# Dealing row pairs to partitions so that the 16 DMA engines read neighbouring pairs, in a mean over rows

## The chip, the cores and the metric

The kernel runs on one core of one Trainium2 chip; the other cores are idle. Times are device microseconds (us) of that core, medians of several executions. The median of before is 1245.4 us (1245.29 to 1245.93 in four runs).

## The reference

```python
"x": np.random.randn(64, 256, 8192).astype(np.float32)
def reference(x): return np.mean(x, axis=2)
```

That is 16384 rows of 32 KiB, 537 MB to read, and 64 KiB of means to write. It is a problem of reading memory.

## The kernel before

A tile is 256 rows: partition p of 128 receives the row pair p of the tile, 64 KiB in one piece. Three buffers in SBUF, the memory on the chip, rotate. SP (SyncE) issues the loads, 16 DMA engines carry them out, DVE (VectorE) sums each row, TensorE transposes the sums at the end into PSUM, its output memory, and ACT (ScalarE) copies them out of there in order. A packet is the piece that one DMA engine moves at a time; the trace records each (8064 of 64 KiB for the full tiles; while they move, 16 are in flight for 97.7% of the time). The last 256 rows come in ever smaller pieces, so that little work is left after the last byte.

```python
P, R, NBUF = 128, 2, 3                     # L = 8192
x_rows = x.rearrange("b c l -> (b c) l")
x_pair = x_rows.rearrange("(t p r) l -> t p (r l)", p=P, r=R)
out_pair = out.rearrange("b c -> (b c)").rearrange("(t n) -> t n", n=R * P)
# ... cut: buffers, semaphores
def sync_program(eng):
    for t in range(NP):                    # NP = 63 full tiles
        if t >= NBUF:
            eng.wait_ge(dve_sem, t - NBUF + 1)
        eng.dma_start(bufs[t % NBUF][:], x_pair[t]).then_inc(in_sems[t % NBUF], 16)
    # ... cut: six loads of the last tile, two stores
def vector_program(eng):
    def pair(k, trip, dst):
        eng.wait_ge(in_sems[k], trip)
        eng.tensor_reduce(dst, bufs[k][:].rearrange("p (r l) -> p r l", r=R), X, ADD
                          ).then_inc(dve_sem, 1)
    # ... cut: the loop over tiles, the last tile
def scalar_program(eng):
    for r in range(R):
        eng.wait_ge(pe_sem, r + 1)
        eng.activation(outsb[:, :, r], ps[r][:], Copy, scale=inv).then_inc(cp_sem, 1)
    # ... cut: the last tile
def tensor_program(eng):
    eng.wait_ge(prep_sem, 4)
    eng.wait_ge(dve_sem, NP + 1)
    for r in range(R):
        eng.transpose(ps[r][:], res[:, :, r], ident[:]).then_inc(pe_sem, 1)
    # ... cut: the last tile
```

Of the kernel before, what the change touches and what calls it, by code (L numbers as in the profile page):

```python
# [6 lines left out]
def bass_global_avg_pool_1d_kernel(  # L7
# [4 lines left out]
    P = 128  # L12
    B, C, L = x.shape
    rows = B * C
    inv = 1.0 / float(L)
# [3 lines left out]
    Copy = mybir.ActivationFunctionType.Copy  # L19



    R = 2
    assert rows % (R * P) == 0
    NP = rows // (R * P) - 1
    NBUF = 3
# [6 lines left out]
    BLOCKS.append((32, [L // 8, 5 * L // 64, 3 * L // 64]))  # L33
    assert sum(n for n, _ in BLOCKS) == R * P
    assert all(sum(ch) * P == n * L for n, ch in BLOCKS)
# [2 lines left out]
    NCH = sum(len(ch) for _, ch in BLOCKS)  # L38

    x_rows = x.rearrange("b c l -> (b c) l")  # L40
    x_pair = x_rows.rearrange("(t p r) l -> t p (r l)", p=P, r=R)
    out_pair = out.rearrange("b c -> (b c)").rearrange("(t n) -> t n", n=R * P)

    with ExitStack() as ctx:
        E = ctx.enter_context
        bufs = [E(nc.sbuf_tensor(f"buf{i}", [P, R * L], f32)) for i in range(NBUF)]
        res = E(nc.sbuf_tensor("res", [P, NP, R], f32))
# [5 lines left out]
        outsb = E(nc.sbuf_tensor("outsb", [NP, P, R], f32))  # L53
        lastsb = E(nc.sbuf_tensor("lastsb", [1, R * P], f32))
        ps = [E(nc.psum_tensor(f"ps{r}", [NP, P], f32)) for r in range(R)]
# [8 lines left out]
        cp_sem = E(nc.semaphore("cp_sem"))  # L64
# [103 lines left out]
        def scalar_program(eng):  # L168

            for r in range(R):  # L170
                eng.wait_ge(pe_sem, r + 1)
                eng.activation(outsb[:, :, r], ps[r][:], Copy, scale=inv).then_inc(cp_sem, 1)  # L172
            at = 0
            for k, (n, _) in enumerate(BLOCKS[:-1]):
                eng.wait_ge(pe_sem, R + 1 + k)
                eng.activation(lastsb[:, at : at + n], psb[k][:, :n], Copy).then_inc(cp_sem, 1)  # L176
                at += n
# [17 lines left out]
        gpsimd_program(nc.gpsimd)  # L195
        vector_program(nc.vector)
        scalar_program(nc.scalar)
        tensor_program(nc.tensor)

# [39 lines left out]
```

## Time and profile before

| | before |
|---|---|
| median time, us | 1245.4 |
| GB/s over the span | 432 |
| one full tile (8.39 MB), us | 19.39 |
| DVE on one full tile, us | 17.22 |
| packets of the full tiles | 8064 of 64 KiB |
| one such packet, mean / median, us | 2.424 / 2.421 |

From the page of before: the busy share of DVE and of the DMA engines in 40 slices (tenths), the rate in each slice, the costliest group of instructions (count, busy us, mean ns, idle time before and what ended it), and the loads (count, median us from issue to landing). Then the shares of the chain of work that ended last.

```profile
DVE  2898988989889888898898988989889898898988
DMA  9999999999999999999999999999999999999998
GB/s 436 415 430 438 438 438 426 417 438 438 438 438 438 436 407 438 438 438 438 438 434 409 438 438 438 438 438 434 409 438 438 438 438 438 432 411 438 438 438 373
DMA packets 10010, 536.94 MB, mean 432 GB/s; under 512 B 1114, under 2 KB 1306, under 8 KB 1562
...
L130 DVE TENSOR_REDUCE res<-buf 128x16384 f32 (+1 forms) x62 | 1067.6, 17220 | 152.4 <-DMA buf<-in_x_dram 152.4
...
buf<-in_x_dram SPq DMA_DIRECT2D x63, 40.7
...
DMA 70%; DVE 29%; issue 0%; SPq 0%; DVEq 0%; PE 0%
```

DMA is busy to the end and DVE idles 152.4 us waiting for it, so the loads bound the kernel. A load lands 40.7 us after its issue, twice a tile's 19.39: one tile always queues behind the one being moved. The dips to 407-417 are no stalls. The trace shows the 16 engines starting their packets within 0.46 us of one another (in 99 of 100 rounds), so bytes arrive in rounds of 16 x 64 KiB, and a slice of 31.1 us counts 12 or 13 of them; 13 rounds make 438 GB/s. Two longer windows (columns: stretch and its length, busy us and instructions of each engine, clock, DMA share, GB/s) show no dip; the second is the last tile:

```profile
400.00:1200.00 800.00, 0.00 (x0) 0.00 (x0) 712.69 (x42) 0.00 (x0) 0.00 (x0) 1.00 1.00 434
1222.10:1242.50 20.40, 2.68 (x14) 0.80 (x14) 18.29 (x16) 1.16 (x5) 0.00 (x0) 1.00 0.92 389
```

### The profile page before, as it was taken

What the parts mean: (1) busy time and instruction counts of PE and PEld (TensorE: products, weight loads), DVE (VectorE), ACT (ScalarE), POOL (GpSimd) and SP (SyncE); (2) the same over time, 40 slices, a digit from 0 to 9 for tenths busy, and PEclk for the clock granted to TensorE, in tenths of its full rate; (3) what the DMA queues carried; (4) which work ended last, traced back from release to release, by engine and by line L of the source; (5) the groups of instructions that cost most, each with busy time, mean ns of one, the idle gap of its engine ahead of it and who ended that gap; (6) DMA issues with size and microseconds to landing.
All of it is one profiled execution on the core that took longest, in us unless ns stands there. A gap on an engine that the chain in (4) does not pass through costs nothing.

```text
span 1243.9 us, 331 instructions
## 1 busy us (share of the span) xinstructions
PE 2.7 (0%) x14; PEld 0.8 (0%) x14; DVE 1086.1 (87%) x79; ACT 2.4 (0%) x6; POOL 1.2 (0%) x8
## 2 busy tenths in 40 slices
PE   0000000000000000000000000000000000000000
PEld 0000000000000000000000000000000000000000
DVE  2898988989889888898898988989889898898988
ACT  0000000000000000000000000000000000000000
POOL 0000000000000000000000000000000000000000
DMA  9999999999999999999999999999999999999998
GB/s 436 415 430 438 438 438 426 417 438 438 438 438 438 436 407 438 438 438 438 438 434 409 438 438 438 438 438 434 409 438 438 438 438 438 432 411 438 438 438 373
DMA packets 10010, 536.94 MB, mean 432 GB/s; under 512 B 1114, under 2 KB 1306, under 8 KB 1562
## 3 DMA queue, kind: packets, MB, share of 16 engines
q1 hardware_dynamic: 10010, 536.94, 99.9%
HBM read 536.87 MB, written 0.07 MB: 432 GB/s over the span
## 4 chain that ended last, share of the span: by engine, by line
DMA 70%; DVE 29%; issue 0%; SPq 0%; DVEq 0%; PE 0%
DMA buf<-in_x_dram 70%; DVE res L130 29%; DVEq L130 0%; SPq L113 0%; DVE buf L137 0%; SPq L109 0%; PE psb L188 0%; DVE lastsb L166 0%; DVE part L137 0%
## 5 line engine op out<-in xcount | busy, mean ns | idle before, releaser
L130 DVE TENSOR_REDUCE res<-buf 128x16384 f32 (+1 forms) x62 | 1067.6, 17220 | 152.4 <-DMA buf<-in_x_dram 152.4
L137 DVE CUSTOM_DVE_ANT_0 buf<-buf 128x4096 f32<-128x4096 f32 (+5 forms) x8 | 18.2, 2292 | 3.9 <-DMA buf<-in_x_dram 3.7
L183 PE MATMUL ps<-ident,res 128*63 128x128 f32 x2 | 0.7, 433 | 1231.1 <-DVE res L137 1231.1
L172 ACT ACTIVATE outsb<-ps 63x128 f32<-63x128 f32 x2 | 0.5, 279 | 1228.5 <-PE ps L183 1228.5
L188 PE MATMUL psb<-ind,part 128*1 128x32 f32 (+1 forms) x10 | 1.4, 238 | 4.1 <-DVE part L137 4.1
L172 ACT ACT_TABLE_LOAD x1 | 1.3, 1283 | 1.7 <-PEq L224 1.7
L183 PEld LDWEIGHTS ps<-ident,res 128*63 128x63 f32 x2 | 0.3, 202 | 1231.0 <-issue 1231.0
L176 ACT ACTIVATE lastsb<-psb 1x128 f32<-1x128 f32 (+2 forms) x3 | 0.7, 222 | 8.3 <-PE psb L188 8.3
L188 PE MATMUL psb<-ident,part 128*1 128x128 f32 x2 | 0.6, 397 | 4.6 <-DVE part L137 4.6
L137 DVE DVE_READ_ACCUMULATOR2_ANT part<- 128x1 f32 x6 | 0.5, 82 | 0.0
L166 DVE COPY lastsb<-psb 1x32 f32<-1x32 f32 x1 | 0.2, 178 | 0.4 <-PE psb L188 0.4
L188 PEld LDWEIGHTS psb<-ind,part 128*1 128x1 f32 x10 | 0.4, 80 | 5.5 <-DVE part L137 5.5
L85 POOL TENSOR_SCALAR_AFFINE_SELECT ident<-ident 128x128 f32<-128x128 f32 x1 | 0.3, 293 | 0.2 <-POOL ident L83 0.2
L95 POOL TENSOR_TENSOR ind<-ident 128x64 f32<-128x64 f32 x1 | 0.3, 291 | 0.1
L99 POOL TENSOR_TENSOR ind<-ind 128x32 f32<-128x32 f32 x1 | 0.2, 238 | 0.1
L83 POOL MEMSET ident<- 128x128 f32 x1 | 0.2, 204 | 1.3 <-POOLq L224 1.3
L137 DVE DVE_READ_ACCUMULATOR2_ANT res<- 128x1 f32 x2 | 0.2, 83 | 0.0
L224 POOL MEMSET const-bfloat16-1.0<- 128x1 bf16 x1 | 0.1, 101 | 0.0
L224 POOL MEMSET const-uint8-127<- 128x1 uint8 x1 | 0.1, 101 | 0.0
L224 POOL MEMSET const-float32-0.0<- 128x1 f32 x1 | 0.1, 98 | 0.2 <-issue 0.2
L224 POOL MEMSET const-float32-1.0<- 128x1 f32 x1 | 0.1, 98 | 0.0
L188 PEld LDWEIGHTS psb<-ident,part 128*1 128x1 f32 x2 | 0.1, 80 | 5.0 <-DVE part L137 5.0
## 6 DMA issues: line engine op xcount, KB each, us to landing
buf<-in_x_dram SPq DMA_DIRECT2D x1, 4096.0 KB, 31.1
buf<-in_x_dram SPq DMA_DIRECT2D x1, 2048.0 KB, 16.7
buf<-in_x_dram SPq DMA_DIRECT2D x1, 1024.0 KB, 18.8
buf<-in_x_dram SPq DMA_DIRECT2D x63, 40.7
buf<-in_x_dram SPq DMA_DIRECT2D x1, 512.0 KB, 19.6
buf<-in_x_dram SPq DMA_DIRECT2D x1, 320.0 KB, 20.0
buf<-in_x_dram SPq DMA_DIRECT2D x1, 192.0 KB, 20.0
out_dram<-outsb SPq DMA_DIRECT2D x1, 63.0 KB
```

The costliest lines, as they stand in the source:

```text
L83: eng.memset(ident[:], 0.0).then_inc(prep_sem, 1)
L85: eng.affine_select(out=ident[:], in_=ident[:], compare_op=mybir.AluOpType.not_equal, fill=1.0, base=0, pattern=[[-1, P]], channel_multipl ...
L95: eng.tensor_tensor(ind64[:], ident[:, 0:P:2], ident[:, 1:P:2], ADD).then_inc(prep_sem, 1)
L99: eng.tensor_tensor(ind32[:], ind64[:, 0:64:2], ind64[:, 1:64:2], ADD).then_inc(prep_sem, 1)
L130: eng.tensor_reduce(dst, bufs[k][:].rearrange("p (r l) -> p r l", r=R), X, ADD).then_inc(dve_sem, 1)
L137: return eng.tensor_tensor_reduce(out=run[:, 0:h], in0=run[:, 0:h], in1=run[:, h:], scale=scale, scalar=0.0, op0=ADD, op1=ADD, accum_out=dst,)
L166: eng.tensor_copy(lastsb[:, EARLY:], psb[-1][:, :n]).then_inc(last_sem, 1)
L172: eng.activation(outsb[:, :, r], ps[r][:], Copy, scale=inv).then_inc(cp_sem, 1)
L176: eng.activation(lastsb[:, at : at + n], psb[k][:, :n], Copy).then_inc(cp_sem, 1)
L183: eng.transpose(ps[r][:], res[:, :, r], ident[:]).then_inc(pe_sem, 1)
L188: mm = eng.matmul(psb[k][:, :n], part[:, i : i + 1], ind[n][:], start=start, stop=stop)
L224: nc = _bacc.Bacc("TRN2", target_bir_lowering=False, num_devices=1)
```

## The change

The intent: at any time the 16 engines should read 16 neighbouring pairs, 1 MiB of memory in one piece. The source pattern therefore deals the pairs as (j, e): partition 8e + j gets pair 16j + e. It supposes that the outer index e goes to the engines. The sums then stand in another order, which the two ACT copies undo.

```diff
     R = 2
+    J = P // 16
@@
-    x_pair = x_rows.rearrange("(t p r) l -> t p (r l)", p=P, r=R)
+    x_pair = x_rows.rearrange("(t j e r) l -> t e j (r l)", j=J, e=16, r=R)
@@
-                eng.activation(outsb[:, :, r], ps[r][:], Copy, scale=inv).then_inc(cp_sem, 1)
+                eng.activation(
+                    outsb[:, :, r].rearrange("t (j e) -> t j e", j=J),
+                    ps[r][:].rearrange("t (e j) -> t j e", j=J),
+                    Copy,
+                    scale=inv,
+                ).then_inc(cp_sem, 1)
```

The load changes from a source of two levels (128 steps of 64 KiB, then 64 KiB in one piece) to one of three: 16 steps of 64 KiB, 8 steps of 1 MiB, 64 KiB in one piece. The destination is the same 128 partitions.

## The prediction

> **What bounds the kernel.** The load queue. The page's busy-share row shows DMA at 9 tenths in every slice but the last; the table by windows gives 433 GB/s in each 19.39 us (one 8.39 MB tile) for nearly the whole run. The records of the DMA packets in the trace say it more sharply: each of the 8064 packets of the 63 full tiles carries 64 KiB (one row pair), the median takes 2.42 us, the shortest 2.415, 97% are below 2.43; that is 27.1 GB/s for each of 16 engines, 433.6 GB/s in all. [...] DVE has slack: 17.22 us a tile against 19.39, and it waited 152.4 us on loads over 62 tiles (table of waits). A load takes 40.7 us from issue to landing, twice the transfer of one tile, so the queue always holds a next tile.
>
> The dips to 407-417 GB/s in the page's row are, I think, counting: the packets of all 16 engines end in rounds of 2.42 us, a slice of 31.1 us holds 12 or 13 rounds, and 13 x 16 x 64 KiB / 31.1 us is 438. Windows of whole tiles show no dips.
>
> **What the change does.** [...] the trace shows them in step (starts within 0.45 us). [...] Bytes, packet size (64 KiB), 16-way split, buffers, waits, DVE and PE work are the same; the instruction order is unchanged on every engine. Two ACT copies (0.279 us each) get a read pattern with a stride of 8; I allow up to 0.3 us more each. Their store is issued at 1232.05, 10.7 us before the last one, so this is off the critical path. The source pattern gets one more dimension; if describing it costs the queue anything, only the first load shows it (my estimate 0 to 0.5 us, against 0.40 us of issue now), the others are issued 40 us ahead.
>
> **What it can win.** Only packet time above the floor. The mean over the full tiles is 2.4236 us against 2.418, so 504 packets per engine hold 2.8 us: 0.6 in the first round (3.1 to 3.35 us each), 0.8 in a patch between about 80 and 220 us (up to 2.63), the rest a uniform 3 to 4 ns. If addresses far apart cause this, the change wins at most 2.8 us (0.2%). [...]
>
> **What it could lose.** [...] A packet of 2.47 us would cost 25 us. I think it unlikely.
>
> **Predicted: 1244.8 us, range 1242.6 to 1248.5.** Chances: faster by over 2%: 0.01; within 2%: 0.95; slower by over 2%: 0.04.
>
> **What would show it.** Right: 19.4 us tiles at 433 GB/s in the windows, median packet 2.418-2.422 us, chain of waits still about 70% DMA, DVE waiting about 152 us. Won by addresses: a first round near 2.5 us and no patch of long packets. Wrong: median packet above 2.45 us, more DVE waiting, or packets not of 64 KiB or not on 16 engines[...].

1244.8 us lies 0.6 us below the 1245.4 of before, out of the 2.8 us that 504 packets for each engine hold above 2.418 us, the lower quartile of the packets in the trace. "Them" in "the trace shows them in step" are the 16 DMA engines.

## The result, and the profile after

The changed kernel computes the right result and takes 2579.8 us (2574.6 to 2581.5 in four runs), 2.0706 times before (95% interval 2.067 to 2.0741). Ratios here are the mean time of one kernel's fast runs over that of the other's of the same rounds, so not quite the ratio of the medians quoted.

The same lines of the page of after:

```profile
DVE  2344353543525344353443534435254352534435
DMA  9999999999999999999999999999999999999999
GB/s 212 212 195 212 212 204 202 212 212 197 209 212 208 198 212 212 199 207 212 212 195 212 212 204 202 212 212 197 209 212 207 199 212 212 202 204 212 212 195 261
DMA packets 10010, 536.94 MB, mean 208 GB/s; under 512 B 1114, under 2 KB 1306, under 8 KB 1562
...
L132 DVE TENSOR_REDUCE res<-buf 128x16384 f32 (+1 forms) x62 | 1067.6, 17220 | 1465.0 <-DMA buf<-in_x_dram 1465.0
...
buf<-in_x_dram SPq DMA_DIRECT2D x63, 104.2
```

The number of packets, the bytes and the DVE work are the same to the digit. The DMA row still reads 9 in every slice: a packet that is being held up counts as busy (the DMA share from 400 to 1200 us is 1.00 at 207 GB/s, and was 1.00 at 434 before). That row tells that the queue never ran dry and nothing of how fast it moved. The rate halved, and DVE's wait on loads grew from 152.4 to 1465.0 us. The packet records of the two traces, worked out for the 64 KiB packets alone, say where all of it is:

| 64 KiB packets, us | count | shortest | median | mean | longest |
|---|---|---|---|---|---|
| before | 8064 | 2.415 | 2.421 | 2.424 | 3.349 |
| after | 8064 | 4.269 | 5.102 | 5.071 | 5.542 |

8064 / 16 makes 504 of them for each engine; 504 x (5.071 - 2.424) = 1334 us, and the spans differ by 2577.7 - 1243.9 = 1333.8 us. Nothing else changed by an amount that matters.

Windows of after, answering to those of before:

```profile
400.00:1200.00 800.00, 0.00 (x0) 0.00 (x0) 344.40 (x20) 0.00 (x0) 0.00 (x0) 1.00 1.00 207
2556.00:2576.30 20.30, 2.68 (x14) 0.80 (x14) 18.28 (x17) 1.16 (x5) 0.00 (x0) 1.00 0.93 391
```

The second line is the first clue. The last tile, whose loads the change did not touch, runs at the old speed (391 against 389 GB/s) in the same execution. Three of its loads send 32, 16 and 8 KiB to each partition, in pieces whose neighbours in memory are neighbouring partitions; the medians of its 16 and 32 KiB packets, 0.615 and 1.218 us, are the same in both traces. So the memory is not slow at large; the slowness goes with the 63 changed loads. It reaches beyond them only at the seam: the first 16 packets of the unchanged loads, 15 of which began while the last changed packets were in flight, took 1.44 to 2.08 us, where before none of that size took more than 1.225.

A caution on the chain of work that ended last. Its summary for after is

```profile
another core or an unknown queue 68%; DVE 28%; DMA 3%; issue 0%; DVEq 0%; SPq 0%; PE 0%
```

No other core took part. The pieces of that chain, in order of time (start, length, what), match DVE's waits for loads (23.3 us in the timeline):

```profile
84.23 17.22 DVE res L132
101.45 23.16 another core or an unknown queue
124.61 0.03 issue
```

The profile failed to name the DMA here; the table of groups did name it (1465.0 us).

### The profile page after: what moved, and what is told of

Read it like the earlier page. It is cut to its first block, busy times and chain, and to the rows that moved or that the text cites. A ratio compares the mean times of both kernels' runs of the same rounds, so it can differ in the third digit from the quotient of the medians.

```text
span 2577.7 us, 331 instructions
## 1 busy us (share of the span) xinstructions
PE 2.7 (0%) x14; PEld 0.8 (0%) x14; DVE 1086.1 (42%) x79; ACT 2.4 (0%) x6; POOL 1.2 (0%) x8
## 4 chain that ended last, share of the span: by engine, by line
another core or an unknown queue 68%; DVE 28%; DMA 3%; issue 0%; DVEq 0%; SPq 0%; PE 0%
DVE res L132 28%; DMA buf<-in_x_dram 3%; DVEq L132 0%; DVEq L151 0%; SPq L115 0%; DVE buf L139 0%; PE psb L195 0%; DVE lastsb L168 0%; DVE part L139 0%
## 5 line engine op out<-in xcount | busy, mean ns | idle before, releaser
L132 DVE TENSOR_REDUCE res<-buf 128x16384 f32 (+1 forms) x62 | 1067.6, 17220 | 1465.0 <-DMA buf<-in_x_dram 1465.0
```

## The experiments

Three theories could make each packet take 5 us. Each is a supposition here, put to the test by the runs below.

- PORTS. The writing side: which partitions the engines write at the same time decides, and the new pattern, with its outermost count of 16, makes some engines hold others up. The author supposed that the changed load writes partitions j, j+8, ..., j+120 together. No trace or run shows it, nor a port.
- ADDRESSES. Engines that read neighbouring pairs, 64 KiB apart, collide in memory. This was the risk that the prediction named.
- FORM. A source of three levels is served slowly as such.

No record of the trace names an engine, so the theories had to be tested through what they predict.

### 1. The form without the order (e1_form)

```diff
-    x_pair = x_rows.rearrange("(t p r) l -> t p (r l)", p=P, r=R)
+    def x_tile(t):
+        return bass.AP(x_rows.tensor, t * R * P * L, [[8 * R * L + L // 2, 16], [R * L, 8], [1, R * L]])
@@
-                eng.dma_start(bufs[t % NBUF][:], x_pair[t]).then_inc(in_sems[t % NBUF], 16)
+                eng.dma_start(bufs[t % NBUF][:], x_tile(t)).then_inc(in_sems[t % NBUF], 16)
```

The step of 512 + 16 KiB is odd on purpose: with exactly 512 KiB the two levels would describe the plain pattern again.

> Three theories. [...] ADDRESSES: engines 64 KiB apart collide in memory. FORM: any three-level source pattern is served at half speed. This run keeps the outer count of 16[...]; nothing is read in the changed order (wrong result on purpose). PORTS and FORM: packets of about 5.0 us, 2550 to 2600 us. ADDRESSES: packets of 2.42 us, 1240 to 1260 us.

Measured: 2578.16 us, ratio 2.0698; mean packet 5.066 us. The result was wrong. The slowness stays without the order of the change: each partition reads at most 240 KiB further on than in before. If the outer steps go to the engines, as the change supposed, these are 528 KiB apart here, and ADDRESSES does not explain the run; the trace does not say who reads what.

```profile
400.00:1200.00 800.00, 0.00 (x0) 0.00 (x0) 344.40 (x20) 0.00 (x0) 0.00 (x0) 1.00 1.00 207
```

### 2. Neighbouring reads in the plain form (e2_near)

```diff
+    def x_tile(t):
+        return bass.AP(x_rows.tensor, t * R * P * L, [[L // 2, P], [1, R * L]])
```

Here and in runs 3 and 4, the load takes `x_tile(t)` in place of `x_pair[t]`, as in run 1; those lines are cut.

> The two-level pattern of before with a pitch of 16 KiB a partition in place of 64[...] (they overlap, so the result is wrong on purpose). ADDRESSES: packets near 5 us, about 2580 us. PORTS and FORM: packets of 2.42 us, 1243 to 1250 us.

Measured: 1245.64 us against 1245.59 for before, ratio 1.000 (0.9971 to 1.0029); mean packet 2.423 us. The result was wrong. Reading closer together costs nothing, and gains nothing either: the longest packet, in the first round, was 3.648 us against 3.349. Two limits: most bytes are read several times here, and no record says which partitions are read at the same time, so how far apart the engines were is not shown; the partitions are 16 KiB apart.

```profile
400.00:1200.00 800.00, 0.00 (x0) 0.00 (x0) 712.71 (x42) 0.00 (x0) 0.00 (x0) 1.00 1.00 434
```

### 3. Three levels, outermost count 128 (e3_outer128)

```diff
+    def x_tile(t):
+        return bass.AP(x_rows.tensor, t * R * P * L, [[L, P], [P * L, R], [1, L]])
@@
-        outsb = E(nc.sbuf_tensor("outsb", [NP, P, R], f32))
+        outsb = E(nc.sbuf_tensor("outsb", [NP, R, P], f32))
```

Cut: the two copies and the store, which follow the new order of outsb.

> A three-level source pattern whose outermost count is 128: partition p gets rows p and p+128 of the tile in packets of 32 KiB; the result is right. FORM: near half speed, about 2500 us. PORTS: full speed[...]; a packet of 32 KiB took 1.218 us in the tail of before, so 504 x 2.436 us and 20 to 30 us of start and tail, 1245 to 1262 us. ADDRESSES: [...]anywhere between.

Measured: 1250.04 us, result right, ratio 1.0036 (1.0007 to 1.0065); the 32 KiB packets took 1.218 us each, so two of them 2.436. FORM falls: three levels are not slow as such.

### 4. The change's intent with an outermost count of 128 (e4_quarters)

```diff
+    Q = 4
+    def x_tile(t):
+        return bass.AP(x_rows.tensor, t * R * P * L, [[L // 2, P], [P * L // 2, Q], [1, L // 2]])
@@
-            for r in range(R):
-                eng.transpose(ps[r][:], res[:, :, r], ident[:]).then_inc(pe_sem, 1)
+            for q in range(Q):
+                eng.matmul(
+                    ps[0][:, q * 64 : (q + 1) * 64], res[:, :, q], ind64[:], start=True, stop=True
+                ).then_inc(pe_sem, 1)
```

Cut: the four sums for each partition in place of two, and the copies out of PSUM.

> Three-level pattern, outermost count 128: each partition gets four pieces of 16 KiB, piece q at q x 2 MiB + p x 16 KiB[...]; two half rows are joined by a matmul at the end and the result is right. PORTS: full speed; a packet of 16 KiB took 0.615 us in the tail of before, so 2016 x 0.615 us and 20 to 30 us, 1250 to 1275 us. ADDRESSES and FORM: about 2500 us.

Measured: 1259.22 us, result right, ratio 1.0109 (1.008 to 1.0139); 0.615 us for a packet of 16 KiB. Here partitions 16 KiB apart in memory read without overlap, at nearly full speed: 428 GB/s from 400 to 1200 us, against 434. How far apart the engines were is again not shown. The 1.1% goes with the smaller packets: 4 x 0.615 = 2.46 us for 64 KiB against 2.42. Over 504 that would be about 19 us, where the spans differ by 13.7; what makes up the rest was not looked into.

A first build, never run, let ACT read PSUM while TensorE still wrote to it. In the kernel that ran, the copies wait for all four matmuls.

### 5. and 6. The partitions of each load by hand (e5_ports4, e6_ports8)

If a load of 16 partitions gives one packet to each engine, the partitions chosen are those that the engines write together while they keep step, whoever takes which. The trace supports that one packet: 441 more loads than in before leave 7056 more packets of 4 bytes, 16 for each load, as if each of 16 engines signalled its end once. Each tile comes in eight such loads of the plain form, over 16 consecutive partitions in run 5 and over every eighth partition in run 6.

```diff
# e5_ports4 against before                       (16 consecutive partitions)
+                for j in range(8):
+                    eng.dma_start(bufs[t % NBUF][16 * j : 16 * j + 16, :], x_pair[t, 16 * j : 16 * j + 16]).then_inc(
+                        in_sems[t % NBUF], 16
+                    )
# e6_ports8 against after                        (partitions j, j+8, ..., j+120)
+    x_pair = x_rows.rearrange("(t j e r) l -> t j e (r l)", j=J, e=16, r=R)
+                for j in range(8):
+                    eng.dma_start(bufs[t % NBUF][j : P : 8, :], x_pair[t, j]).then_inc(
+                        in_sems[t % NBUF], 16
+                    )
# both: DVE waits for 128 in place of 16 for each round of a buffer
```

> Each tile comes in eight loads of 16 consecutive partitions (plain two-level pattern, one packet of 64 KiB per engine and load, memory read in the order of the changed kernel, result right). [...] PORTS: [...]9.7 us a packet; [...]at best about 5.2: 2650 to 4900 us. If only memory order or the form mattered, 2.42 us a packet and 1250 us (FORM) or the same as the next run (ADDRESSES, already refuted by the runs before).

> The same eight loads of 16 partitions, same order in memory, plain two-level pattern, but load j goes to partitions j, j+8, ..., j+120, which is the placement that theory PORTS supposes of the changed kernel[...]. Result right, with the reordering copies of the changed kernel. PORTS: 4.9 to 5.1 us a packet and 2500 to 2600 us, as the changed kernel[...]. If the slowness sat in the three-level form: 2.42 us and about 1250 us.

Measured: 4742.23 us (ratio 3.8078) and 2577.78 us (ratio 2.0698), both with right results. Both read memory in the order of the changed kernel. The window from 400 to 1200 us of e5_ports4, and then of e6_ports8:

```profile
400.00:1200.00 800.00, 0.00 (x0) 0.00 (x0) 172.79 (x11) 0.00 (x0) 0.00 (x0) 1.00 1.01 113
```

```profile
400.00:1200.00 800.00, 0.00 (x0) 0.00 (x0) 344.40 (x20) 0.00 (x0) 0.00 (x0) 1.00 1.00 207
```

The rates are 113 GB/s for 16 consecutive partitions and 207 for every eighth, against 434 in before. The 9.7 us expected of run 5 (four times the 2.42 of a packet in before), or 5.2 at best, were an estimate; its packets took 9.318 us. The 64 KiB packets of e6_ports8 are also spread like those of after: 2003 between 4.5 and 5.0 us and 6053 between 5.0 and 5.5, against 2006 and 6052. The placement that PORTS supposes, made by hand, thus reproduces the changed kernel's time and its packets. The two runs read the same memory in the same order with loads of the same size, so the placement in SBUF alone makes 113 or 207 GB/s. Neither has a fast partner: no run found loads of 16 partitions that go at full speed. Run 9 supplies what is missing here, the slow form made fast.

### 7. Seven inner steps in place of eight (e7_seven)

```diff
+    def x_tile(t):
+        return bass.AP(x_rows.tensor, t * R * P * L, [[8 * R * L, 16], [R * L, 7], [1, R * L]])
# loads and sums use 112 partitions; res is cleared once
```

> The slow form (outermost count 16)[...]; an eighth of the bytes of the full tiles is left out, wrong result on purpose. The packets are as large as before[...]. PORTS[...]: a mixture, about half of the packets at 2.42 us and the others at 3 to 5.5, mean about 4.0, so 441 x 4.0 and 20 to 30 us: 1650 to 1850 us. If the outermost count of 16 itself slowed each packet: all packets near 5 us and about 2250 us. If nothing slowed them: about 1110 us.

Measured: 2132.06 us: a miss for both numbers. Packets had a mean of 4.748 us; 3% lay below 3.2 and 2% above 5.5. In the first 150 us the mean was 4.41; from 450 to 1200 us it was about 4.87, with nine packets in ten between 4.54 and 5.11. That is nearer to the 5 us of "the form slows each packet" than to the 4.0 of PORTS, and the 216 GB/s of that stretch is nearly the 207 of after. The 4.0 was the author's estimate, from a model of partial sharing that no run here shows. Why the packets settle at 4.87 us was not tested. By itself the run does not separate PORTS from "this form is slow", which is why the next three were made.

### 8. to 10. The same loads, with a lag between the engines

If packets are slow only because of what the engines write at the same time, then a lag of a few packets between the engines that hold one another up must remove the slowness, with every load of the stream unchanged. The lag is made once, behind the first tile, by extra loads over fewer than 16 partitions, which should give packets to some engines and none to others. Which engines are to fall behind was supposition; the 10 us of lag in the expectation of run 9 are the eight packets of 1.22 us that an engine gets at most. To leave room for the lag, tiles are one row deep with six buffers; e8_rows is that kernel alone.

```diff
# e8_rows against after
-    R = 2
+    R = 1
-    NP = rows // (R * P) - 1
-    NBUF = 3
+    NP = rows // (R * P) - 2
+    NBUF = 6
# (cut: the stores and the last waits, fitted to one row for each partition)
# e9_skew against e8_rows; e10_skew_same has [8] in place of [12, 4], four loads and a wait for 64
+                if t == NBUF - 1:
+                    eng.wait_ge(skew_sem, 128)
                 eng.dma_start(bufs[t % NBUF][:], x_pair[t]).then_inc(in_sems[t % NBUF], 16)
+                if t == 0:
+                    for i in range(8):
+                        n = [12, 4][i // 4]
+                        eng.dma_start(bufs[NBUF - 1][i : i + 9 * n - 8 : 9, :], x_rows[0:n, :]).then_inc(
+                            skew_sem, 16
+                        )
```

The data of the extra loads lie in the sixth buffer and are overwritten; the wait keeps that safe. The traces bear the number of engines out, though not which they are: run 5 had 16 packets of 4 bytes for each load of 16 partitions; e9_skew has 64 more packets of 4 bytes than e8_rows, 4 x 12 + 4 x 4, and e10_skew_same has 32, 4 x 8.

> Ground for the next two runs: the changed kernel with tiles of one row (packets of 32 KiB, 126 tiles, six buffers in place of three, so that fast engines may run further ahead of slow ones); same slow form, same order of reading by neighbours, result right. PORTS and every other theory: half speed as the changed kernel, about 2540 to 2620 us, packets of about 2.5 us in place of 1.218.

> The same kernel, with small extra loads behind the first tile[...]; nothing else differs. [...] PORTS: most packets at 1.22 us; 126 x 8 x 1.22 us, 10 us of lag and 30 us of start and tail: 1260 to 1300 us if the lag lasts, up to 1500 if it erodes. If the form[...] is slow in itself: 2540 to 2630 us as without the extra loads.

> Control: four extra loads[...]. PORTS: no help, 2540 to 2630 us, packets near 2.5 us. If any lag between engines helped, far less.

Measured, all with right results:

| run | median us | ratio to before | mean 32 KiB packet, us |
|---|---|---|---|
| e8_rows | 2552.53 | 2.0496 | 2.502 |
| e9_skew | 1334.28 | 1.0714 | 1.293 |
| e10_skew_same | 2557.16 | 2.0534 | 2.502 |

Windows of e8_rows (one), then of e9_skew, then of e10_skew_same:

```profile
200.00:400.00 200.00, 0.00 (x0) 0.00 (x0) 86.86 (x10) 0.00 (x0) 0.00 (x0) 1.00 1.00 209
```

```profile
200.00:400.00 200.00, 0.00 (x0) 0.00 (x0) 172.91 (x21) 0.00 (x0) 0.00 (x0) 1.00 1.01 419
600.00:800.00 200.00, 0.00 (x0) 0.00 (x0) 171.82 (x21) 0.00 (x0) 0.00 (x0) 1.00 1.00 417
900.00:1100.00 200.00, 0.00 (x0) 0.00 (x0) 170.98 (x20) 0.00 (x0) 0.00 (x0) 1.00 1.00 413
```

```profile
200.00:400.00 200.00, 0.00 (x0) 0.00 (x0) 86.52 (x11) 0.00 (x0) 0.00 (x0) 1.00 1.00 209
600.00:800.00 200.00, 0.00 (x0) 0.00 (x0) 86.50 (x11) 0.00 (x0) 0.00 (x0) 1.00 1.00 209
900.00:1100.00 200.00, 0.00 (x0) 0.00 (x0) 86.50 (x11) 0.00 (x0) 0.00 (x0) 1.00 1.00 209
```

Eight extra loads of at most 12 packets each, 64 packets in all, doubled the rate (419 GB/s against 209) of the loads behind them, which were left word for word as they were, but not every choice does it: with four extra loads over 8 partitions, 32 packets, the rate stayed at 209. The form of the full tiles' loads, their partitions and their addresses are the same in all three; what differs is the extra packets, and so how far some engines are when others are at a given packet. That holds for memory as well as for SBUF, so this pair of runs speaks for a rate that depends on how the engines stand to one another (419 or 209 GB/s); that the writing side matters comes from runs 5 and 6, which read the same memory (113 or 207). Which engines matter to which was not shown.

The 1334 us lie above the 1260 to 1300 expected for a lag that lasts: in place of 1.22 us the packets took 1.258 at 200 us, and 1.274 at 1000 to 1050 us (the rate falls from 419 to 413 GB/s), which reads as a lag that is not exact and erodes; no record shows the lag itself. The first tile, before the lag, still went at half speed (2.44 us a packet), and from 1290 us on packets took over 2 us again. Over 1.218 us, the packets of each engine hold 77 us in all: 18 before 40 us, 45 up to 1250 us, and 13 after it. Why the end slows was not tested.

## Why the prediction was wrong

It said 1244.8 us, 95% within 2%, and the change took 2579.8.

- **What bounds the kernel** was read rightly: the loads, with the engines busy throughout (DMA share 1.00 from 400 to 1200 us), with 2.8 us at most to win by its own sum, which no run tested. The explanation of the dips as counting holds: in after a slice of 64.4 us holds 12 or 13 rounds, and 13 x 16 x 64 KiB / 64.4 us is the 212 of its GB/s row, 12 rounds the 195.
- **A collision of neighbouring reads in memory** was the risk named, and being slower by over 2% was given 4%. Runs 1, 2 and 4 speak against it as the cause: slow without the order of the change (207 GB/s), fast with partitions 16 KiB apart (434 and 428). Runs 5 and 6 read the changed kernel's order alike and differ by placement alone.
- **The step that failed: "Bytes, packet size (64 KiB), 16-way split, buffers, waits, DVE and PE work are the same".** Bytes, packets, buffers and work were. The split was 16-way still (16 packets in flight for 97.8% of the time in after, 97.7% in before). But the changed load has the time and the packets of run 6, where loads of 16 partitions wrote every eighth partition together (207 GB/s), and loads of its form ran at 419 behind the extra packets of run 9. The reading is that what the engines write at the same time changed; no record names the engine of a packet, so this itself was not seen. The prediction did not ask which partitions the engines write at one time. The missing term measured 2.648 us a packet, 504 times.
- **What an engine reads at one time**, before and after, was supposition: no trace or run shows it. That the plain and the new load are dealt to the engines differently is the reading that fits all runs but the size of run 7.
- **The small terms were right.** The issue of a load went from 0.328 to 0.536 us (median), within the 0 to 0.5 allowed, and the strided ACT copies took 278 ns in place of 279, where up to 0.3 us more was allowed. They did not matter.
- **No gain from neighbours.** Loads whose partitions lie 16 KiB apart in memory, in packets of the same size (run 2, 1245.64 us), take the time of before (1245.59), where they lie 64 KiB apart, so closer reads were worth nothing there. Those reads overlap, and who reads what at one time is not shown; so no fast run of 64 KiB packets is known to have read 16 neighbours in one piece.

Why a packet takes 2.09 times as long in after (5.071 us) and not 2.00, in run 5 3.85 times (9.318 us) and not 4, and why run 7 settled where it did, stays open. So does what sets these paces. None of the versions beats before.

## What to carry to other kernels

A rearranged source pattern can halve the rate of a load whose bytes, packets and destination stay the same (207 against 434 GB/s); that it changes which partitions each DMA engine writes, and when, is the reading of the runs here. The loads that kept an outermost count of 128 on both sides, whether the inner levels were plain or reordered, ran at 428 to 434 GB/s (before and runs 2 to 4), and those with 16 outermost at 207 (after and run 1), unless extra packets came before them (run 9: 413 to 419, in rows); so try the first. When a rate halves while packets, bytes and busy shares stay the same, look at the time of one packet and ask who shares what at that moment. A load that covers all 128 partitions over its whole length can still run at the 207 GB/s of loads over every eighth partition (run 6).
